# Eleven orders of the long and short products in group B of a hybrid encoder layer

## The chip, the core and the metric

The kernel runs on one core of one Trainium2 chip. The metric is the time of one execution on the device in microseconds (us); less is better. The kernel before takes 1112.13 us, the median of 3 runs (1111.66 to 1113.59).

## What is computed

One encoder layer for 256 tokens of width 2048. The input projection has nine parts of 2048 columns each; five feed group A (a gated linear recurrence), four feed group B (a short gated convolution). Cut to what matters here:

```python
hn = _rmsnorm(h, norm_w[i])                      # (256, 2048)
proj = hn @ w_in[i]                              # (2048, 9 * 2048)
q, v, f_fwd, f_bwd, z_a, b_gate, c_gate, h_b, z_b = jnp.split(proj, IN_SPLITS, axis=-1)
o_a = ...                                        # group A, from q, v, f_fwd, f_bwd, z_a
y_b = b_gate * _short_conv(c_gate * h_b, conv_w[i])
o_b = _rmsnorm(y_b, conv_norm_w[i]) * jax.nn.silu(z_b)
h = h + jnp.concatenate([o_a, o_b], axis=-1) @ w_out[i]
gate = jax.nn.sigmoid(h @ w_ple_gate[i])
h = h + (p[i] @ w_ple[i]) * gate
return _rmsnorm(h, final_norm_w)
```

## The kernel before, in words

**Products in two parts.** Every float32 matrix product is made of three products of the shorter type float32r. Both operands are split into a high part (a rounded copy) and a low part (what the rounding lost): for the weights ScalarE (ACT) makes the high part (L121) and VectorE (DVE) the low part (L122), 1024 elements of each partition at a time, into a buffer called `spl`. The activations `xs` hold high and low parts side by side, 256 columns each.

**Long and short products.** In `gemm_part` (L417 to L430) the weights are the stationary operand. For each tile of 128 inner rows (a k-tile, `kt`) and each half `m` of 256 output columns there are two matmuls. The long one (L427) has the high weights stationary and streams both parts of `xs`, 512 columns. The short one (L425) has the low weights stationary and streams the high part alone, 256 columns. Both add into the accumulator `acc[m]`, one bank of PSUM each; the short one adds to its first 256 columns. Each matmul loads its own 128x128 weights (LDWEIGHTS, on the row PEld of the profile).

**Column blocks.** `gemm_in` (L432) makes one column block: 256 columns of one part, 16 k-tiles in four groups of four (`g`, one `spl` buffer each), so 32 long and 32 short products, here called 32 pairs. Group B (L924 to L984) has 32 column blocks: for `i` from 0 to 7, one each of `B_CG`, `B_HB`, `B_BG` and `B_ZB`, named CG0, HB0, BG0, ZB0, CG1 and so on below. In all these are 1024 pairs. After each block `evac` (L482) reads the two accumulators with ACT and DVE; there are four accumulator banks, so that the next block goes on in the two others. GpSimd (POOL) and DVE do the convolution and the gates beside it.

**Order.** The order of the matmuls is that in which the program writes them. The usual order of the four products of a k-tile is PLAIN: long 0, short 0, long 1, short 1 (the number is `m`), so that long and short alternate all along. Two other orders stand at single k-tiles of some blocks, by the table TURNED: k-tile 1 by OUTER (long 0, short 0, short 1, long 1) and k-tile 3 by SHORTS (short 0, short 1, long 0, long 1). In group B TURNED stands at CG0, HB0, BG0, ZB0, CG2, CG4, CG6 and ZB6; group A has it too, and its first block has the same two orders at k-tiles 9 and 11 (LATER).

```python
PLAIN = ((0, 0), (0, 1), (1, 0), (1, 1))
OUTER = ((0, 0), (0, 1), (1, 1), (1, 0))
SHORTS = ((0, 1), (1, 1), (0, 0), (1, 0))
TURNED = {1: OUTER, 3: SHORTS}
LATER = {9: OUTER, 11: SHORTS}
```

Some small matmuls of group A's last heads stand between products of group B: those of the outputs (L797, L798) in CG0 after 24 pairs and in BG0 after 28, and the scores (L735, L779) between HB0 and BG0. Before group B stand the products of V and Z_A (`avz`, L547 to L549), which are all 512 columns long; after it those of the output projection, and last those of the gate (`pg`, L1026 to L1028), which have 512 columns, then 512 and 256 in threes, then 256 alone.

**What feeds the matmuls.** SP issues the loads of `w_in`, 1 MB each, into three buffers `raw`; ACT and DVE split them into five buffers `spl`, up to three groups ahead of the matmuls (`Stream.get`). GpSimd's queue meanwhile makes sums of parts of `w_out` in DRAM (`pump`).

Of the kernel before, what the change touches and what calls it, by code (L numbers as in the profile page):

```python
# [17 lines left out]
P = 128  # L18
D = 2048
T = 256  # L20
NKT = D // P
# [4 lines left out]
B_Q, B_V, B_FF, B_FB, B_ZA, B_BG, B_CG, B_HB, B_ZB = (8 * i for i in range(9))  # L26
# [111 lines left out]
def tile_hymba_encoder(  # L138
# [15 lines left out]
    act, dve, pool, pe = nc.scalar, nc.vector, nc.gpsimd, nc.tensor  # L154
# [16 lines left out]
    ws = Stream(tc, rawp, splp, 3)  # L171
# [5 lines left out]
    blocks = {}  # L177
# [31 lines left out]
    for u in range(2):  # L209
        for half in range(2):  # L210
            oblocks.append([])
            for q in ORDER:
                k = 16 * half + 2 * q
# [133 lines left out]
    def pump():  # L347
        if steps_up:
            n, step = steps_up.pop(0)
            add_up(prepared[n], step)  # L350
            if step == 2 and n + 4 < len(prepared):
                prepare(prepared[n + 4])

    def tick():
        now[0] += 1
        due = sorted(e for e in pend if e[0] <= now[0])
        for e in due:
            pend.remove(e)
        for e in due:
            e[2]()  # L360
# [3 lines left out]
    xs = xsp.tile([P, NKT, 2, T], F32R, name="xs")  # L364
# [42 lines left out]
    def acc_in(c, i):  # L407
        return [psg.tile([P, 2, T], F32, tag="g", name=f"a{c}_{i}_{m}") for m in range(2)]
# [5 lines that stand above are left out]
    TURNED = {1: OUTER, 3: SHORTS}  # L414
    LATER = {9: OUTER, 11: SHORTS}

    def gemm_part(acc, w, g, k0=0, k1=4, orders={}):  # L417

        for k in range(k0, k1):
            kt = 4 * g + k  # L420
            for m, short in orders.get(kt, PLAIN):
                a = acc[m].rearrange("p a b -> p (a b)")
                lhsT = w[:, k, short, m * P : (m + 1) * P]
                if short:
                    pe.matmul(a[:, :T], lhsT=lhsT, rhs=xs[:, kt, 0, :], start=False, stop=(kt == NKT - 1))  # L425
                else:
                    pe.matmul(  # L427
                        a, lhsT=lhsT, rhs=xs[:, kt, :, :].rearrange("p s n -> p (s n)"), start=(kt == 0), stop=False
                    )
            tick()  # L430

    def gemm_in(c, i, orders={}):  # L432

        acc = acc_in(c, i)
        for g in range(4):
            gemm_part(acc, ws.get(blocks[c, i][g]), g, orders=orders)
        return acc

    def gemm_two(c, i, dst):
# [42 lines left out]
    def evac(acc, dst, tmpp, offset=200):  # L482

        with tc.high_priority(offset=offset):
            for m in range(2):
                r = tmpp.tile([P, T], F32, tag="r", name="r", bufs=2)
                act.copy(out=r, in_=acc[m][:, 1, :])  # L487
                dve.tensor_tensor(out=dst(m), in0=acc[m][:, 0, :], in1=r, op=ALU.add)

    def by_norms(t, r, n):  # L490

        pool.tensor_tensor(out=t, in0=t, in1=r.unsqueeze(1).broadcast_to([P, n, T]), op=ALU.mult)  # L492


    first = (B_FF, B_FB, B_Q)
# [3 lines left out]
    with tc.manual_schedule(engines={ENG.Activation, ENG.DVE, ENG.PE}):  # L499
        for g in range(4):  # L500
            for c in range(3):
                half, v = ws.open(ids3[c][g])

                n = 2 if g or c else 1
# [24 lines left out]
    def act_sums(src, a, s, place=lambda instr: instr):  # L529


        place(dve.tensor_tensor(out=a, in0=src[:, :, 0], in1=src[:, :, 1], op=ALU.add))
        a11, a21, a12, a22 = (a[:, k, m * P : (m + 1) * P] for k in range(2) for m in range(2))
        for o, x, y in ((0, a21, a22), (1, a21, a11), (2, a11, s[:, 0]), (3, a12, s[:, 2])):
            dve.tensor_tensor(out=s[:, o], in0=x, in1=y, op=ALU.subtract)

    def act_split(dst, src, s):

        n = dst.shape[1]
        for d, r in ((dst, s[:, 0:n]), (src[:, 0:1, :, P:], s[:, n:])):  # L540
            if r.shape[1]:
                act.copy(out=d[:, :, 0], in_=r)
                dve.tensor_tensor(out=d[:, :, 1], in0=r, in1=d[:, :, 0], op=ALU.subtract)
# [374 lines left out]
    ctmp = bctx.enter_context(tc.tile_pool(name="ctmp", bufs=1, side="left", reuse_waits="tile"))  # L918
# [2 lines left out]
        pool.memset(t, 0.0)  # L921
    ysum = ctmp.tile([P, 2, T], F32, name="ysum")
    pool.memset(ysum, 0.0)
    for i in range(8):  # L924
        cg = ctmp.tile([P, 2, T], F32, tag="cg", name=f"cg{i}", bufs=2)
        evac(gemm_in(B_CG, i, TURNED if i % 2 == 0 else {}), lambda m: cg[:, m, :], ctmp)
        hb = ctmp.tile([P, 2, T], F32, tag="hb", name=f"hb{i}", bufs=2)
        evac(gemm_in(B_HB, i, {} if i else TURNED), lambda m: hb[:, m, :], ctmp)
        u = ub[i % 2]
        by_norms(cg, rbc2, 2)  # L930
        pump()
        pool.tensor_tensor(out=u[:, :, 1 : T + 1], in0=cg, in1=hb, op=ALU.mult)
        pump()
        for m in range(2):
            ct = 2 * i + m
            dve.tensor_scalar(cg[:, m, :], u[:, m, 0:T], cvw[:, 0, ct : ct + 1], None, op0=ALU.mult)
            for j in (1, 2):
                dve.scalar_tensor_tensor(
                    out=cg[:, m, :], in0=u[:, m, j : j + T], scalar=cvw[:, j, ct : ct + 1],
                    in1=cg[:, m, :], op0=ALU.mult, op1=ALU.add,  # L940
                )
        evac(gemm_in(B_BG, i, {} if i else TURNED), lambda m: hb[:, m, :], ctmp)
        pool.tensor_tensor(out=cg, in0=cg, in1=hb, op=ALU.mult)
        pump()
        y2 = ctmp.tile([P, 2, T], F32, tag="tmp", name=f"y2_{i}")
        act.activation(y2, cg, AF.Square)
        pool.tensor_tensor(out=ysum, in0=ysum, in1=y2, op=ALU.add)
        pump()
        evac(gemm_in(B_ZB, i, TURNED if i in (0, 6) else {}), lambda m: hb[:, m, :], ctmp)
        by_norms(hb, rbc, 2)  # L950
        pump()
        sz = ctmp.tile([P, 2, T], F32, tag="tmp", name=f"szb{i}")
        act.activation(sz, hb, AF.Sigmoid)
        for m in range(2):
            ct = 2 * i + m
            dve.scalar_tensor_tensor(
                out=hb[:, m, :], in0=hb[:, m, :], scalar=cnw[:, ct : ct + 1], in1=sz[:, m, :],
                op0=ALU.mult, op1=ALU.mult,
            )
        pool.tensor_tensor(out=cg, in0=cg, in1=hb, op=ALU.mult)  # L960
        pump()
        if i == 0:
            assert not pend
            actx.close()
            bp = mctx.enter_context(tc.tile_pool(name="bp", bufs=1, side="right", reuse_waits="tile"))
            mixb = bp.tile([P, NH, 2, T], F32R, name="mixb")
            og = bp.tile([P, 2, 2, 2, P], F32, name="og")
            suma = bp.tile([P, len(SUMS), 3, 2, P], F32R, name="suma")
        if i == 2:
            for e in range(2):  # L970
                act.copy(out=og[:, e], in_=kept[e])
        hi, lo = mixb[:, 2 * i : 2 * i + 2, 0, :], mixb[:, 2 * i : 2 * i + 2, 1, :]
        act.copy(out=hi, in_=cg)
        dve.tensor_tensor(out=lo, in0=cg, in1=hi, op=ALU.subtract)
        for src, z, n in ((mixa, i - 1, len(SUMS)), (mixb, i - SUMS[0], len(sumb32))):
            if 0 <= z < n:
                k = 2 * SUMS[z]
                a = ctmp.tile([P, 2, T], F32, tag="tmp", name=f"sa{i}")
                if src is mixb:
                    act_sums(mixb[:, k : k + 2], a, sumb32[z])  # L980
                else:
                    t = ctmp.tile([P, 4, P], F32, tag="hb", name=f"sb{i}", bufs=2)
                    act_sums(mixa[:, k : k + 2], a, t)
                    act_split(suma[:, z], mixa[:, k : k + 2], t)  # L984
# [22 lines left out]
    hh = hp.tile([P, 2, D], F32, name="hh")  # L1007
# [43 lines left out]
    def four(pool_, name):  # L1051
        if pool_ is psg:
            return [psg.tile([P, 512], F32, tag="g", name=f"{name}_{b}") for b in range(4)]
        return [psm.tile([P, 512], F32, tag=t, name=f"{name}_{t}") for t in FOUR]
# [8 lines left out]
    for u in range(2):  # L1063
# [9 lines left out]
        for src, sums, main, other, scale in ((mixa, suma, psg, psm, False), (mixb, sumb, psm, psg, True)):  # L1073
            name = f"p{'ab'[scale]}{u}"
            acc = four(main, name)
            parts = oblocks[2 * u + scale]
            if u == 0 and not scale:
                for z in range(len(SUMS)):
                    k = 2 * SUMS[z]
# [5 lines left out]
            for q1, q5, q6, q7 in half([acc[0:2], acc[2:4]], extra, ORDER, SUMS, parts, src, sums, False):  # L1085
                d, v, d7, v7 = tmps
# [179 lines left out]
```

## Time and profile before

| what | value |
|---|---|
| median of 3 runs | 1112.13 us (1111.66 to 1113.59) |
| the profiled execution: time, span | 1112.2 us, 1110.5 us |
| TensorE (PE) busy | 1100.5 us, 99% of the span |
| weight loads (PEld) busy | 945.7 us, 85% |
| VectorE, ScalarE, GpSimd busy | 851.4, 677.3, 269.1 us |
| mean granted clock of TensorE | 0.998 of full speed |
| chain of waits, share of PE | 98% |

The span is the time from the first to the last instruction that the profile shows; 1.7 us of the profiled execution lie around it. A matmul's row in the profile has a start and a duration; since matmuls are pipelined, durations overlap, and what a product costs in a row of them is the time from its start to the next one's start. The order of instructions is told by lists of each engine, the times by the trace.

### The profile page before, as it was taken

To read this page: it belongs to the slowest core of one execution; us is meant where nothing else is said; L and a number is where in the kernel's file an instruction comes from. 1 tells how busy PE (TensorE), PEld (TensorE's weight loads), DVE (VectorE), ACT (ScalarE), POOL (GpSimd) and SP (SyncE) were. 2 spreads that over 40 slices of the span, in tenths; PEclk is the share of its full clock that TensorE was granted. 3 is DMA by queue.
4 is the path that set the end of the run, shared out by engine and by line. 5 is a ranking of instruction groups with operands and counts; after the bars stand their busy time and mean duration, and the time that the engine had idled before them with its cause. 6 is when DMAs were issued, how large, how long until landed. Compare 5 with 4: busy or idle time off the path is not lost.

```text
span 1110.5 us, 16882 instructions
## 1 busy us (share of the span) xinstructions
PE 1100.5 (99%) x6455; PEld 945.7 (85%) x6455; DVE 851.4 (77%) x1127; ACT 677.3 (61%) x946; POOL 269.1 (24%) x215
## 2 busy tenths in 40 slices
PE   9999999999999999999999999999999999999997
PEld 8888888888888888888888888888888888888886
DVE  7799578896889778997657758856667888887673
ACT  6786577667876697575545535535546575575562
POOL 1045015203530325043334223424331000000101
PEclk9999999999999999999999999999999999999999
DMA  9755454564457744758999998999979887887542
GB/s 340 272 187 190 153 190 157 171 242 153 161 162 258 292 152 152 231 172 228 298 310 250 270 334 231 282 345 254 288 196 306 318 299 286 286 312 253 193 133 76
DMA packets 69808, 260.44 MB, mean 235 GB/s; under 512 B 7008, under 2 KB 16608, under 8 KB 52192
## 3 DMA queue, kind: packets, MB, share of 16 engines
q1 hardware_dynamic: 60480, 242.25, 62.1%
q0 software_dynamic: 8960, 16.78, 10.0%
q8 instruction: 51, 0.84, 0.3%
q10 hardware_dynamic: 288, 0.34, 0.1%
q14 instruction: 29, 0.24, 0.1%
HBM read 257.25 MB, written 35.65 MB: 264 GB/s over the span
## 4 chain that ended last, share of the span: by engine, by line
PE 98%; DMA 1%; ACT 0%; SPq 0%; DVE 0%; DVEq 0%; issue 0%; ACTq 0%
PE a L427 37%; PE a L425 19%; PE avz L547 3%; PE avz L548 3%; PE avz L549 3%; PE pg L1027 3%; PE pg L1026 3%; PE pg L1028 3%; PE pa L547 2%; PE pa L548 2%; PE pa L549 2%; PE a L446 1%; PE a L448 1%; PE a L447 1%; PE pb_sc L548 1%; PE pb_sc L549 1%
## 5 line engine op out<-in xcount | busy, mean ns | idle before, releaser
L122 DVE TENSOR_TENSOR spl<-raw,spl 128x1024 fp32r<-128x1024 f32 (+2 forms) x419 | 505.0, 1219 | 163.6 <-ACT spl L121 160.2
L427 PE MATMUL a<-xs,spl 128*128 128x512 f32 x1792 | 617.3, 395 | 0.6 <-ACT spl L121 0.6
L121 ACT CAST spl<-raw 128x1024 fp32r<-128x1024 f32 (+2 forms) x419 | 414.1, 999 | 255.0 <-PE a L425 81.9
L425 PE MATMUL a<-xs,spl 128*128 128x256 f32 x1792 | 483.8, 278 | 0.0
L427 PEld LDWEIGHTS a<-xs,spl 128*128 128x128 f32 x1792 | 332.2, 188 | 73.6 <-ACT spl L121 1.0
L425 PEld LDWEIGHTS a<-xs,spl 128*128 128x128 f32 x1792 | 334.6, 188 | 5.8 <-DVE spl L122 0.5
L1143 POOL TENSOR_TENSOR hh<-hh,fw 128x512 f32<-128x512 f32 (+1 forms) x9 | 11.0, 1227 | 250.7 <-ACT gt L1142 248.0
L487 ACT COPY r<-a 128x256 f32<-128x256 f32 x112 | 40.5, 368 | 37.3 <-PE a L425 35.8
L547 PE MATMUL avz<-spl,xs 128*128 128x512 f32 x138 | 54.0, 391 | 0.0
L549 PE MATMUL avz<-spl,xs 128*128 128x512 f32 x138 | 53.7, 389 | 0.0
L548 PE MATMUL avz<-spl,xs 128*128 128x512 f32 x138 | 53.7, 389 | 0.0
L1026 PE MATMUL pg<-spl,ht 128*128 128x512 f32 (+1 forms) x120 | 45.2, 377 | 0.0
L1027 PE MATMUL pg<-spl,ht 128*128 128x512 f32 (+1 forms) x120 | 45.1, 376 | 0.0
L1028 PE MATMUL pg<-spl,ht 128*128 128x512 f32 (+1 forms) x120 | 45.0, 375 | 0.0
L716 POOL TENSOR_TENSOR qc<-pf,ge 128x256 f32<-128x256 f32 x16 | 18.3, 1148 | 105.8 <-ACT dd L706 91.8
L492 POOL TENSOR_TENSOR xf<-xf,rbc 128x1024 f32<-128x1024 f32 x8 | 19.9, 2486 | 94.0 <-DVE rbc L403 50.2
L121 ACT CAST spl<-early 128x1024 fp32r<-128x1024 f32 (+1 forms) x29 | 28.7, 990 | 19.1 <-PE pb_y L549 7.5
L122 DVE TENSOR_TENSOR spl<-early,spl 128x1024 fp32r<-128x1024 f32 (+1 forms) x29 | 32.9, 1147 | 9.2 <-ACT spl L121 8.8
L547 PE MATMUL pa<-spl,mixa 128*128 128x512 f32 x88 | 34.5, 392 | 0.0
L549 PE MATMUL pa<-spl,mixa 128*128 128x512 f32 x88 | 34.3, 389 | 0.0
L548 PE MATMUL pa<-spl,mixa 128*128 128x512 f32 x88 | 34.2, 389 | 0.0
L716 POOL TENSOR_TENSOR kc<-dd,ge 128x256 f32<-128x256 f32 x16 | 27.7, 1728 | 19.8 <-DVE dd L707 13.6
(321 smaller groups left out, 1641.7 us busy)
## 6 DMA issues: line engine op xcount, KB each, us to landing
raw<-in_w_in_dram SPq DMA_DIRECT2D x106, 1024.0 KB, 6.9
raw<-in_w_in_dram SPq DMA_DIRECT2D x100, 256.0 KB, 3.9
raw<-in_w_out_dram SPq DMA_DIRECT2D x36, 512.0 KB, 5.2
sums<-in_w_out_dram SPq DMA_DIRECT2D x32, 512.0 KB, 10.6
raw<-in_w_in_dram SPq DMA_DIRECT2D x26, 512.0 KB, 5.2
raw<-sums SPq DMA_DIRECT2D x13, 1024.0 KB, 5.3
raw<-in_w_gate_dram SPq DMA_DIRECT2D x9, 1024.0 KB, 5.1
sums<-in_w_out_dram POOLq DMA_DIRECT2D x16, 512.0 KB, 10.1
```

The source lines that it names most:

```text
L121: self.nc.scalar.copy(out=v[:, :, 0], in_=r)
L122: self.nc.vector.tensor_tensor(out=v[:, :, 1], in0=r, in1=v[:, :, 0], op=ALU.subtract)
L425: pe.matmul(a[:, :T], lhsT=lhsT, rhs=xs[:, kt, 0, :], start=False, stop=(kt == NKT - 1))
L427: pe.matmul(a, lhsT=lhsT, rhs=xs[:, kt, :, :].rearrange("p s n -> p (s n)"), start=(kt == 0), stop=False)
L487: act.copy(out=r, in_=acc[m][:, 1, :])
L547: pe.matmul(acc, lhsT=ah, rhs=w[:, 0], start=start, stop=False)
L548: pe.matmul(acc, lhsT=ah, rhs=w[:, 1], start=False, stop=False)
L549: pe.matmul(acc, lhsT=al, rhs=w[:, 0], start=False, stop=stop)
L716: pool.tensor_tensor(out=c64(dst[:, d]), in0=c64(src[:, d, :, half * P : (half + 1) * P]), in1=g.unsqueeze(3).broadcast_to([P, 2, 2, CH]), ...
L1026: pe.matmul(acc[m], lhsT=lh, rhs=wh, start=(kt == 0), stop=False)
L1027: pe.matmul(acc[m], lhsT=lh, rhs=wl, start=False, stop=False)
L1028: pe.matmul(acc[m], lhsT=ll, rhs=wh, start=False, stop=(kt == nk - 1))
```

## The change

`gemm_part` no longer walks k-tile by k-tile with one of the three orders; it takes a list of all 16 products of a group of four k-tiles, made by `products_of` for one of eleven styles, named by letters a to k. The string STYLES gives each column block of group B its style: in turn one plain block and two blocks of one style, from CG0 (plain), HB0 and BG0 (a), ZB0 (plain), CG1 and HB1 (b), to HB7 (j), BG7 (plain) and ZB7 (k). TURNED is no longer used in group B; group A keeps it. `tick()` still comes after every four products, and the `stop` flag at the last product of each accumulator.

With L and S for long and short, the styles are: a: L0 L1 S0 S1 in each k-tile; b: L0 S1 L1 S0; c: L0 L1 S1 S0; d: in each group of four k-tiles all eight longs, then all eight shorts; e: in each group first `m` 0, then `m` 1, long and short in turn; f: in each group for each `m` four longs, then four shorts; g: by two k-tiles four longs, then four shorts; h: as d, but shorts first in the second and third groups; i: OUTER in each k-tile; j: S0 L0 S1 L1; k: SHORTS. In b, i, j and k the first and last k-tile of a block stay plain.

```diff
+    L0, S0, L1, S1 = PLAIN
+    BY_TILE = {
+        "a": (L0, L1, S0, S1), "b": (L0, S1, L1, S0), "c": (L0, L1, S1, S0),
+        "i": OUTER, "j": (S0, L0, S1, L1), "k": SHORTS,
+    }
+
+    def products_of(style, g, k0, k1, orders):
+        ks = range(k0, k1)
+        if style in ("d", "h"):
+            kinds = (1, 0) if style == "h" and 0 < g < 3 else (0, 1)
+            return [(k, m, short) for short in kinds for k in ks for m in range(2)]
+        if style == "e":
+            return [(k, m, short) for m in range(2) for k in ks for short in range(2)]
+        if style == "f":
+            return [(k, m, short) for m in range(2) for short in range(2) for k in ks]
+        if style == "g":
+            return [(k, m, short) for kk in (k0, k0 + 2) for short in range(2) for k in (kk, kk + 1) for m in range(2)]
+        plain = BY_TILE.get(style, PLAIN)
+        first = PLAIN if style in ("b", "i", "j", "k") else plain
+        return [(k, *o) for k in ks for o in orders.get(4 * g + k, plain if 0 < 4 * g + k < 15 else first)]
...
+        todo = products_of(style, g, k0, k1, orders)
...
+    STYLES = " aa bb cc dd ee ff gg hh ii jj k".ljust(32)
     for i in range(8):
         cg = ctmp.tile([P, 2, T], F32, tag="cg", name=f"cg{i}", bufs=2)
-        evac(gemm_in(B_CG, i, TURNED if i % 2 == 0 else {}), lambda m: cg[:, m, :], ctmp)
+        evac(gemm_in(B_CG, i, style=STYLES[4 * i + 0]), lambda m: cg[:, m, :], ctmp)
         hb = ctmp.tile([P, 2, T], F32, tag="hb", name=f"hb{i}", bufs=2)
-        evac(gemm_in(B_HB, i, {} if i else TURNED), lambda m: hb[:, m, :], ctmp)
+        evac(gemm_in(B_HB, i, style=STYLES[4 * i + 1]), lambda m: hb[:, m, :], ctmp)
...
-        evac(gemm_in(B_BG, i, {} if i else TURNED), lambda m: hb[:, m, :], ctmp)
+        evac(gemm_in(B_BG, i, style=STYLES[4 * i + 2]), lambda m: hb[:, m, :], ctmp)
...
-        evac(gemm_in(B_ZB, i, TURNED if i in (0, 6) else {}), lambda m: hb[:, m, :], ctmp)
+        evac(gemm_in(B_ZB, i, style=STYLES[4 * i + 3]), lambda m: hb[:, m, :], ctmp)
```

In the changed kernel the long product stands at L450 and the short one at L448. The numbers of instructions are the same on every engine; on PE the products of group B stand in another order, on DVE and ACT eight instructions have changed places with a neighbour, and on POOL and SP nothing has moved.

The first place is PE at the start of CG0, the products of its first two k-tiles; in a48_0_1, 48 is the part CG, 0 the `i`, and 1 the half `m`; 128x512 is a long and 128x256 a short product. Before:

```order
L427 MATMUL a48_0_0_4603<-xs_174,spl178_4532 128x512
L425 MATMUL a48_0_0_4603<-xs_174,spl178_4532 128x256
L427 MATMUL a48_0_1_4604<-xs_174,spl178_4532 128x512
L425 MATMUL a48_0_1_4604<-xs_174,spl178_4532 128x256
L427 MATMUL a48_0_0_4603<-xs_174,spl178_4532 128x512
L425 MATMUL a48_0_0_4603<-xs_174,spl178_4532 128x256
L425 MATMUL a48_0_1_4604<-xs_174,spl178_4532 128x256
L427 MATMUL a48_0_1_4604<-xs_174,spl178_4532 128x512
```

The second k-tile is turned (OUTER): two shorts stand in a row, then the last long, and the next product, of the third k-tile, is a long too. Now:

```order
L450 MATMUL a48_0_0_4603<-xs_174,spl178_4532 128x512
L448 MATMUL a48_0_0_4603<-xs_174,spl178_4532 128x256
L450 MATMUL a48_0_1_4604<-xs_174,spl178_4532 128x512
L448 MATMUL a48_0_1_4604<-xs_174,spl178_4532 128x256
L450 MATMUL a48_0_0_4603<-xs_174,spl178_4532 128x512
L448 MATMUL a48_0_0_4603<-xs_174,spl178_4532 128x256
L450 MATMUL a48_0_1_4604<-xs_174,spl178_4532 128x512
L448 MATMUL a48_0_1_4604<-xs_174,spl178_4532 128x256
```

CG0 now alternates from its first product to its last. The second place is PE in the first group of BG2 (part 40), one of the two blocks of style d. Now, from the fifth product on:

```order
L450 MATMUL a40_2_0_5703<-xs_174,spl218_5628 128x512
L450 MATMUL a40_2_1_5704<-xs_174,spl218_5628 128x512
L450 MATMUL a40_2_0_5703<-xs_174,spl218_5628 128x512
L450 MATMUL a40_2_1_5704<-xs_174,spl218_5628 128x512
L448 MATMUL a40_2_0_5703<-xs_174,spl218_5628 128x256
L448 MATMUL a40_2_1_5704<-xs_174,spl218_5628 128x256
L448 MATMUL a40_2_0_5703<-xs_174,spl218_5628 128x256
L448 MATMUL a40_2_1_5704<-xs_174,spl218_5628 128x256
```

Eight longs are followed by eight shorts (four of each are shown); before, this block alternated throughout. Counted over all of group B, there were 16 places where two or more shorts stand in a row, and as many with longs in a row, two of each for every TURNED; now there are 154 of each: 16 in each block of a and c, 4 in d, 8 in f and g, 3 in h, 14 in i and k, 1 in j, none in b, e and the plain ones.

## Rows read from the trace of the kernel before

**Rows 1.** The page: span, busy time of each engine, chain of waits by engine.

```profile
span 1110.5 us, 16882 instructions
...
PE 1100.5 (99%) x6455; PEld 945.7 (85%) x6455; DVE 851.4 (77%) x1127; ACT 677.3 (61%) x946; POOL 269.1 (24%) x215
...
PE 98%; DMA 1%; ACT 0%; SPq 0%; DVE 0%; DVEq 0%; issue 0%; ACTq 0%
```

**Rows 2.** Busy time by engine in group B: us, busy (count), granted clock, DMA.

```profile
474.00:836.00 362.00, 362.00 (x2180) 317.14 (x2178) 252.10 (x337) 180.84 (x260) 126.09 (x102) 1.00 0.91 265
```

**Rows 3.** Groups of instructions, 474 to 836 us: busy, mean ns, idle before, releasers.

```profile
L427 PE MATMUL a<-xs,spl 128*128 128x512 f32 x1024 | 353.6, 394 | 0.0
L425 PE MATMUL a<-xs,spl 128*128 128x256 f32 x1024 | 279.9, 277 | 0.0
...
L121 ACT CAST spl<-raw 128x1024 fp32r<-128x1024 f32 x129 | 134.4, 1050 | 103.2 <-PE a L425 65.4 <-DMA raw<-in_w_in_dram 30.4 <-PE a L427 3.7
```

**Rows 4.** Timeline of PE, plain blocks of group B: start, duration, instruction.

```profile
580.64 0.40 PE L427 MATMUL a<-xs,spl 128*128 128x512 f32 x1
...
602.83 0.40 PE L427 MATMUL a<-xs,spl 128*128 128x512 f32 x1
```

**Rows 5.** Timeline of PE, plain k-tiles of the kernel's first blocks.

```profile
14.69 0.40 PE L427 MATMUL a<-xs,spl 128*128 128x512 f32 x1
...
15.39 0.40 PE L427 MATMUL a<-xs,spl 128*128 128x512 f32 x1
15.63 0.28 PE L425 MATMUL a<-xs,spl 128*128 128x256 f32 x1
...
25.29 0.40 PE L427 MATMUL a<-xs,spl 128*128 128x512 f32 x1
```

**Rows 6.** Timeline of PE around one TURNED in group B.

```profile
657.61 0.40 PE L427 MATMUL a<-xs,spl 128*128 128x512 f32 x1
...
658.18 0.39 PE L425 MATMUL a<-xs,spl 128*128 128x256 f32 x2
...
660.40 0.40 PE L427 MATMUL a<-xs,spl 128*128 128x512 f32 x1
```

**Rows 7.** Timeline of PE, from the products of V and Z_A into CG0.

```profile
473.43 0.39 PE L549 MATMUL avz<-spl,xs 128*128 128x512 f32 x1
473.65 0.39 PE L427 MATMUL a<-xs,spl 128*128 128x512 f32 x1
...
474.35 0.40 PE L427 MATMUL a<-xs,spl 128*128 128x512 f32 x1
474.59 0.40 PE L425 MATMUL a<-xs,spl 128*128 128x256 f32 x2
```

**Rows 8.** Timeline of PE in BG0 and ZB0, after the small matmuls of the outputs.

```profile
511.95 0.40 PE L427 MATMUL a<-xs,spl 128*128 128x512 f32 x1
...
513.69 0.39 PE L427 MATMUL a<-xs,spl 128*128 128x512 f32 x1
```

**Rows 9.** Timeline of PE in the gate: products of 512 columns alone.

```profile
1061.83 0.39 PE L1026 MATMUL pg<-spl,ht 128*128 128x512 f32 x1
...
1076.11 0.39 PE L1026 MATMUL pg<-spl,ht 128*128 128x512 f32 x1
```

**Rows 10.** Timeline of PE in the gate: three of 512, three of 256, in turn.

```profile
1081.68 0.40 PE L1026 MATMUL pg<-spl,ht 128*128 128x512 f32 x1
...
1087.98 0.40 PE L1026 MATMUL pg<-held,ht 128*128 128x512 f32 x1
```

**Rows 11.** Timeline of PE in the gate: products of 256 columns alone.

```profile
1096.75 0.28 PE L1026 MATMUL pg<-spl,ht 128*128 128x256 f32 x1
...
1099.15 0.28 PE L1028 MATMUL pg<-spl,ht 128*128 128x256 f32 x1
...
1099.63 0.28 PE L1026 MATMUL pg<-held,ht 128*128 128x256 f32 x1
...
1101.75 0.28 PE L1026 MATMUL pg<-held,ht 128*128 128x256 f32 x1
```

More of the change, by code (lines that the diff above doesn't have):

```diff
@@ L415, in tile_hymba_encoder @@
     LATER = {9: OUTER, 11: SHORTS}
-    def gemm_part(acc, w, g, k0=0, k1=4, orders={}):
-        for k in range(k0, k1):
-            kt = 4 * g + k
[L421 to L430, printed above, removed]
@@ L432, in gemm_in @@
-    def gemm_in(c, i, orders={}):
+    L0, S0, L1, S1 = PLAIN
[17 more added lines that the diff above has]
+        return [(k, *o) for k in ks for o in orders.get(4 * g + k, plain if 0 < 4 * g + k < 15 else first)]
@@ new lines, in gemm_part @@
+    def gemm_part(acc, w, g, k0=0, k1=4, orders={}, style=""):
+        todo = products_of(style, g, k0, k1, orders)
+        last = {m: max(n for n, o in enumerate(todo) if o[1] == m) for m in range(2)}
+        for n, (k, m, short) in enumerate(todo):
+            kt = 4 * g + k
+            a = acc[m].rearrange("p a b -> p (a b)")
+            lhsT = w[:, k, short, m * P : (m + 1) * P]
+            stop = g == 3 and k1 == 4 and n == last[m]
+            if short:
+                pe.matmul(a[:, :T], lhsT=lhsT, rhs=xs[:, kt, 0, :], start=False, stop=stop)
+            else:
+                pe.matmul(
+                    a, lhsT=lhsT, rhs=xs[:, kt, :, :].rearrange("p s n -> p (s n)"), start=(kt == 0), stop=stop
+                )
+            if n % 4 == 3:
+                tick()
@@ L434, in gemm_in @@
+    def gemm_in(c, i, orders={}, style=""):
         acc = acc_in(c, i)
         for g in range(4):
-            gemm_part(acc, ws.get(blocks[c, i][g]), g, orders=orders)
+            gemm_part(acc, ws.get(blocks[c, i][g]), g, orders=orders, style=style)
         return acc
```

## The prediction

> **What bounds the kernel now.** I read the page first. TensorE is busy for 1100.5 of the 1110.5 us of the span, and 98% of the chain of waits is PE [rows 1]. So the time is the sum of what the products cost, one after the other, wherever PE does not wait. The busy time by stretches shows the same of group B alone: from 474 to 836 us PE is busy for all 362.00 us, at a granted clock of 1.00, with DVE at 252.10, ACT at 180.84 and POOL at 126.09 us [rows 2]. The list of instruction groups says who is ahead: ACT, which makes the high parts of the weights, idles 103.2 us in this stretch, and 65.4 us of it end when a short product frees a buffer [rows 3]. The splits wait for PE, not PE for them: neither kind of product has any idle time before it. A change in the order of products therefore acts on the time by one thing only: the time from each product's start to the next one's.
>
> The timeline of PE gives that time, and the reader should see that it is not one number. In plain blocks of group B, 64 pairs of a long and a short product take 22.19 us, 0.3467 us a pair [rows 4]. In the kernel's first blocks, with the same lines, shapes and order and 30 pairs without a wait, a pair takes 10.60/30 = 0.3533 us, and at times a short starts 0.24 us after its long (15.39 to 15.63) [rows 5]. So alternation has a **tight pace** and a **loose pace**, 6.6 ns a pair apart, and PE stays in either for as long as nothing disturbs it.
>
> **The change part by part.** It adds and removes no instruction, and leaves the queues of SP and POOL as they were, so loads and sums are issued in the same order. Eight neighbours that change places on DVE and ACT cost nothing while PE does not wait for either; if that cover went, one split of 1050 ns [rows 3] would be the size of a stall. Blocks of style h read the low halves first in two groups, and these come from DVE, after ACT's; the splits are held back by full buffers, so they lie there already. I cost this at 0. In d and h both accumulators end within the last two shorts; the next block uses the other two banks, so a later read of one delays nobody on PE. What stays are two terms.
>
> *Term 1, runs.* Places with two or more longs and shorts in a row (one run of each I call a cycle) go from 16 to 154, so 138 more. Alone, each kind is cheap: 63 long products take 14.28 us, 0.2267 each [rows 9], and shorts take 2.40/20 = 0.1200 or 2.12/18 = 0.1178 each [rows 11]. Sum of one each: 0.3445 to 0.3467, as in the tight pace or slightly less. What costs is the passage from one kind to the other. Where three of 512 and three of 256 columns take turns, 18 pairs take 6.30 us, 0.3500 a pair [rows 10]: 3.3 ns over the tight pace, 10 ns a cycle of three pairs. One TURNED holds two cycles; 8 pairs across it take 2.79 us against 8 x 0.3467 = 2.773 [rows 6], 17 ns, with the rounding of the two starts 7 to 27 ns, so 3 to 14 ns a cycle. Bounds: 0 (the price of runs alone) and 14 ns; a gain of 2.2 ns a pair is taken up as a rival. I take 10 ns, the row nearest to what is added, a steady turn of runs: 138 x 10 = **1.38 us**. The eight TURNED that go are in it, with 16 cycles.
>
> *Term 2, the pace of alternation.* Seventeen blocks still alternate throughout or nearly: the eleven plain ones and those of b, e and j, 544 pairs. Before, eight TURNED stood in their way. CG0 comes out of the products of V and Z_A, a row of longs, and its third long already takes 0.24 us (474.35 to 474.59), as in the loose pace, just ahead of the turned k-tile [rows 7]. Without it I expect CG0's first 24 pairs to stay loose, up to the small matmuls of the outputs: 24 x 6.6 ns = **0.16 us**. After such matmuls the products of BG0 and ZB0 went on at 1.74/5 = 0.348 us a pair [rows 8], near the tight pace, so the eight pairs of CG0's rest cost nothing. For the other 512 pairs the entry decides, and each comes from a new order: ZB0 to BG1 (128 pairs, out of a), HB2, CG3 to ZB3 (128, out of d), BG4, HB5, CG6, and ZB6 to BG7 (128, out of i). No row shows alternation that follows these orders. The bounds are 0 and 512 x 6.6 ns = 3.4 us. Of the two undisturbed entries that I have, one went loose [rows 7] and one near tight [rows 8], so I take half: **1.7 us**.
>
> A rule of the Trainium skill, of the page "TensorE: Matmul & The Clock Gate" (section "Back-to-back issue gap"), speaks against all of this: at full clock the gap of an isolated matmul is its columns over 2.4 GHz and 2.5 ns, whatever stands beside it. By it a pair takes an estimated 215.8 + 109.2 = 325 ns in any order, and the sum of the change is 0. The trace does not bear out the size (346.7 ns) nor that columns alone decide [rows 4, 5].
>
> The sum is 1.38 + 0.16 + 1.7 = 3.2 us. The profiled execution took 1112.2 us, 1.7 more than its span and 0.1 over the median of the runs, 1112.13. 1112.2 + 3.2 = **1115.4 us**, 0.3% slower.
>
> **The rivals.**
>
> *All entries tight.* The runs put PE in the tight pace as TURNED did. For it: a TURNED ends in a run of three longs, and the 64 pairs that I read as tight [rows 4] lie behind the one of CG2. Against it: CG0 comes out of a run of longs and is loose [rows 7], so the length or the moment of a run counts. Then only 1.38 + 0.16 us are left: 1113.7 us. It decides where fewer than about 100 of the 512 pairs are loose (below 2.2 us in all).
>
> *Order is free.* Each product costs what its columns cost in steady rows, passages come to nothing, and every entry is tight; this would be the page's rule with another constant. For it: 0.2267 + 0.1200 us of runs alone make just the 0.3467 of alternation [rows 4, 9, 11]. Against it: 0.3500 a pair where runs take turns [rows 10]. The eight TURNED give back 8 x 17 ns = 0.14 us: 1112.1 us, no slower than before. It holds if a cycle costs under 2 ns and no stretch is loose.
>
> *All entries loose, dear cycles.* 138 x 14 ns = 1.93, 0.16 and 3.4 us: 1117.7 us. For it: nothing in group B would set the pace right any more, and a loose stretch lasted for 30 pairs by itself [rows 5].
>
> *Runs are cheaper.* In long runs a pair may cost 0.3445 us [rows 9, 11], 2.2 ns less than in the tight pace. On the 256 pairs of d, f, g and h this gives 0.56 us, with the 0.14 of TURNED 0.7 us: 1111.5 us. For a gain that shows, the 480 pairs of all run styles would have to save 4.6 ns each; no row has that.
>
> That the change does not do what it says is no rival: the list of PE's instructions shows each style in its block.
>
> **How the numbers follow.** A measurement of this kernel tells about 0.2% (2.2 us) from no change, so the limit is about 1114.3 us. I give my forecast, a part of the entries loose, 0.42; all loose 0.16; both end above the limit, together 0.58 for slower. All entries tight has 0.28 and order is free 0.10, both within 0.2%; of the 0.04 of cheaper runs 0.01 stays within, so 0.39 for the same and 0.03 for faster. The predicted time is that of the forecast. The range goes from the free order, 1112.0, over the bounds of both terms to all loose, 1117.7 with 0.3 for the rounding of the rows: 1112.0 to 1118.0 us. This leaves out cheaper runs, and stalls that I cost at nothing.
>
> **What would show it.** Term 1: in blocks of a, c, f and g a pair takes near 0.350 us, and PE has no idle time before L448 and L450; at 0.3467 it was free, above 0.3515 (14 ns on a cycle of three pairs) too low. Term 2: CG0's first 24 pairs take 8.48 us instead of 8.32; plain blocks take either 11.09 or 11.31 us for 32 pairs, some of each, and a stretch keeps its pace to its end. If all take 11.09 us, the first rival holds. The prediction is wrong in kind if PE waits for a split or a load in group B, if the granted clock falls, or if the blocks of a style take a third price well outside 0.3445 to 0.3533 us a pair.

## The result and the profile after

The changed kernel takes 1115.93 us, the median of 9 runs (1115.16 to 1116.53); the kernel before, beside it, 1112.13 us (9 runs, 1111.24 to 1114.01). The ratio is 1.0031, with a 95% interval of 1.0021 to 1.0042: 3.8 us slower. The profiled execution took 1116.53 us, 4.3 more than that of the kernel before (1112.2).

The page of the changed kernel, the lines that answer to [rows 1]:

```profile
span 1114.7 us, 16881 instructions
...
PE 1104.2 (99%) x6455; PEld 947.9 (85%) x6455; DVE 854.2 (77%) x1127; ACT 676.5 (61%) x946; POOL 264.6 (24%) x215
...
PE 96%; DMA 1%; DVE 1%; ACT 1%; SPq 0%; issue 0%; POOL 0%; DVEq 0%; ACTq 0%
```

The span grew by 4.2 us and PE's busy time by 3.7, with the same 6455 matmuls. The busy time of group B, read to 840 us because it ends 3.4 us later now (columns as in [rows 2]), and then the groups of instructions of that stretch (columns as in [rows 3]):

```profile
474.00:840.00 366.00, 366.00 (x2180) 320.04 (x2179) 253.88 (x339) 180.86 (x260) 123.69 (x102) 1.00 0.90 263
```

```profile
L450 PE MATMUL a<-xs,spl 128*128 128x512 f32 x1023 | 328.5, 396 | 0.0
L448 PE MATMUL a<-xs,spl 128*128 128x256 f32 x1023 | 234.7, 280 | 0.0
...
L121 ACT CAST spl<-raw 128x1024 fp32r<-128x1024 f32 x129 | 134.3, 1051 | 108.6 <-PE a L448 53.3 <-DMA raw<-in_w_in_dram 33.1 <-PE a L450 22.0
```

The reader is to see that nothing new waits. PE is busy for all 366.00 us, the granted clock is 1.00 (the level of 2.4 GHz) as before, neither kind of product has idle time ahead of it, and ACT still idles until a product frees a buffer; in part it is now a long one (22.0 us, before 3.7), since in several styles a long ends a group. The 2048 products themselves stand further apart. From the first product of group B to its last it is 364.82 us, before 361.06: 3.76 of the 4.2 us. The rest of the program behind them takes 0.84 us more; what lies ahead, 0.36 less.

The timeline of PE of the changed kernel gives the paces: start, duration, instruction, and how often it follows itself.

```profile
512.81 0.40 PE L450 MATMUL a<-xs,spl 128*128 128x512 f32 x1
...
524.12 0.40 PE L450 MATMUL a<-xs,spl 128*128 128x512 f32 x1
...
558.04 0.62 PE L450 MATMUL a<-xs,spl 128*128 128x512 f32 x2
...
569.19 0.63 PE L450 MATMUL a<-xs,spl 128*128 128x512 f32 x2
...
580.34 0.40 PE L450 MATMUL a<-xs,spl 128*128 128x512 f32 x1
...
591.43 1.99 PE L450 MATMUL a<-xs,spl 128*128 128x512 f32 x8
593.25 1.11 PE L448 MATMUL a<-xs,spl 128*128 128x256 f32 x8
594.21 1.32 PE L450 MATMUL a<-xs,spl 128*128 128x512 f32 x5
...
602.59 0.40 PE L450 MATMUL a<-xs,spl 128*128 128x512 f32 x1
...
658.99 1.08 PE L450 MATMUL a<-xs,spl 128*128 128x512 f32 x4
659.91 0.64 PE L448 MATMUL a<-xs,spl 128*128 128x256 f32 x4
...
670.20 0.40 PE L450 MATMUL a<-xs,spl 128*128 128x512 f32 x1
```

From each block's first long to the next block's first: ZB0 (plain) 524.12 - 512.81 = 11.31 us, 0.3534 a pair, the loose pace to its last pair; HB2 (plain, the same products in the same order) 591.43 - 580.34 = 11.09 us, the tight pace of [rows 4]; ZB1 (c, runs of two) 11.15; BG2 (d, runs of eight) 11.16, and one cycle of it, 591.43 to 594.21, 2.78 us; CG4 (f, runs of four) 11.21. All 32 blocks, by the starts of their products, in ns a pair:

| blocks | ns a pair |
|---|---|
| CG0, first 24 pairs | 352.8 |
| a: HB0, BG0; c: ZB1, CG2 | 348.7, 348.4; 348.3, 348.3 |
| plain ZB0, BG1; b: CG1, HB1 | 353.5, 353.5; 353.1, 353.4 |
| plain HB2, BG4, HB5 | 346.7, 346.8, 346.8 |
| d: BG2, ZB2; h: BG5, ZB5 | 348.6, 349.2; 348.6, 348.5 |
| plain CG3, ZB3; e: HB3, BG3 | 353.5, 353.5; 353.1, 353.4 |
| f: CG4, HB4; g: ZB4, CG5 | 350.3, 350.8; 350.7, 350.8 |
| plain CG6, ZB6, BG7 | 353.5, 353.4, 353.5 |
| i: HB6, BG6; k: ZB7 | 349.0, 348.9; 348.7 |
| j: CG7, HB7 | 347.6, 353.0 |

**The sum from it.** Twelve blocks are loose: 384 pairs x 6.67 ns = 2.56 us. CG0 adds 0.15 in its first 24 pairs and 0.05 in its last eight, which are loose too (352.6 ns a pair). The blocks in runs, with CG7, stand over 32 x 346.67 ns by 1.21 us in all. The eight TURNED of the kernel before cost 0.26 us by the same count. 2.56 + 0.15 + 0.05 + 1.21 - 0.26 = 3.71 of the 3.76 us.

**Behind group B.** The waits of PE in the output projection show one stop that the kernel before does not have, a product behind a split whose load of `w_out` landed late; then the timeline of PE there:

```profile
PE pa L572 <- DVE spl L122: 0.5, 1, 0.5
```

```profile
859.99 0.39 PE L571 MATMUL pa<-spl,mixa 128*128 128x512 f32 x1
860.90 0.50 PE L572 MATMUL pa<-spl,mixa 128*128 128x512 f32 x1 [0.52 <-DVE spl L122]
861.24 0.39 PE L573 MATMUL pa<-spl,mixa 128*128 128x512 f32 x1
```

From 859.99 to 860.90 it is 0.91 us, where such a product takes 0.23: some 0.7 of the 0.84 us.

### The profile page after: what moved, and what is told of

It is laid out like the page before. It is cut to its first block, busy times and chain, and to the rows that moved or that the text cites. A ratio compares the mean times of both kernels' runs of the same rounds, so it can differ in the third digit from the quotient of the medians.

```text
span 1114.7 us, 16881 instructions
## 1 busy us (share of the span) xinstructions
PE 1104.2 (99%) x6455; PEld 947.9 (85%) x6455; DVE 854.2 (77%) x1127; ACT 676.5 (61%) x946; POOL 264.6 (24%) x215
## 4 chain that ended last, share of the span: by engine, by line
PE 96%; DMA 1%; DVE 1%; ACT 1%; SPq 0%; issue 0%; POOL 0%; DVEq 0%; ACTq 0%
PE a L450 37%; PE a L448 19%; PE avz L573 3%; PE avz L571 3%; PE avz L572 3%; PE pg L1052 3%; PE pg L1051 3%; PE pg L1053 3%; PE pa L572 1%; PE pa L573 1%; PE pa L571 1%; PE a L470 1%; PE a L471 1%; PE a L472 1%; PE pb_sc L573 1%; PE pb_sc L572 1%
## 5 line engine op out<-in xcount | busy, mean ns | idle before, releaser
L450 PE MATMUL a<-xs,spl 128*128 128x512 f32 x1792 | 592.7, 396 | 0.5 <-ACT spl L121 0.5
L448 PE MATMUL a<-xs,spl 128*128 128x256 f32 x1792 | 438.8, 279 | 0.2 <-DVE spl L122 0.2
L450 PEld LDWEIGHTS a<-xs,spl 128*128 128x128 f32 x1792 | 323.0, 188 | 62.7 <-ACT spl L121 0.8
L448 PEld LDWEIGHTS a<-xs,spl 128*128 128x128 f32 x1792 | 324.5, 188 | 18.0 <-DVE spl L122 0.5
```

The costliest lines, as they stand in the source:

```text
L450: pe.matmul(a, lhsT=lhsT, rhs=xs[:, kt, :, :].rearrange("p s n -> p (s n)"), start=(kt == 0), stop=stop)
```

## The experiments

The theory: PE alternates at one of several paces, the entry decides which, and the change pays for loose entries and, by a smaller sum, for runs. The rivals: TURNED had no part in it; the styles' runs alone cost the time; one kind of entry always gives one pace. Group B is told from its first product to its last; before takes 361.06 us there. "Pair" and "cycle" are those of the prediction.

**e1_no_turned**: the kernel before, TURNED taken out of group B, no style put in.

```diff
-        evac(gemm_in(B_CG, i, TURNED if i % 2 == 0 else {}), lambda m: cg[:, m, :], ctmp)
+        evac(gemm_in(B_CG, i), lambda m: cg[:, m, :], ctmp)
```

and the same for HB, BG and ZB.

> The kernel before with TURNED taken out of group B and nothing put in its place: all 32 blocks alternate. Theory (the pace of alternation is set by the moment at which PE enters it, and holds until the order is broken): CG0 comes out of a run of longs, so its first 24 pairs take 0.3533 us each (8.48 us, not 8.32). Small matmuls break in after these, between HB0 and BG0, and in BG0; behind the last of them 29 blocks follow without a break, from ZB0 to ZB7, and all must have one pace: either 11.09 us each, and the time is 1112.1 us, or 11.31 us each, 6.2 us more, 1118.1 us. Rival 1 (loose pairs come from what runs beside PE, the DMA traffic or the reads of the accumulators): the pace changes within these 29 blocks, and is loose at about the times at which it was in the changed kernel (512 to 558, 614 to 659, 748 to 760, 782 to 793, 804 to 827 us): 1114 to 1115 us. Rival 2 (loose pairs are the after-effect of the new orders alone): all blocks at 11.09 us, CG0 too, 1111.9 us.

Measured: 1113.6 us (10 runs), ratio 1.0007 (0.9993 to 1.0021); group B 364.16 us. CG0's first 24 pairs are loose, 352.8 ns each, so is HB0 (353.6), as TURNED's absence was to make them. But out of the small matmuls in BG0 comes a **third pace**: 230.0 ns from each long to its short and 116.7 from there to the next long, where the tight pace has 231.8 and 114.8; the sum is 346.67 in both. I call it the even pace. It holds for fourteen blocks, and then turns loose without any change of order. The timeline of this kernel at that place, all engines, and then the first longs of ZB4 and of ZB7:

```profile
674.24 1.22 DVE L122 TENSOR_TENSOR spl<-raw,spl 128x1024 fp32r<-128x1024 f32 x1
...
675.05 0.39 PE L427 MATMUL a<-xs,spl 128*128 128x512 f32 x1
675.05 0.19 PEld L425 LDWEIGHTS a<-xs,spl 128*128 128x128 f32 x1
...
675.28 0.28 PE L425 MATMUL a<-xs,spl 128*128 128x256 f32 x1
...
675.39 0.39 PE L427 MATMUL a<-xs,spl 128*128 128x512 f32 x1
...
675.51 0.19 PEld L425 LDWEIGHTS a<-xs,spl 128*128 128x128 f32 x1
675.63 0.28 PE L425 MATMUL a<-xs,spl 128*128 128x256 f32 x1
...
679.76 1.21 DVE L122 TENSOR_TENSOR spl<-raw,spl 128x1024 fp32r<-128x1024 f32 x1
...
680.95 0.39 PE L427 MATMUL a<-xs,spl 128*128 128x512 f32 x1
...
681.02 0.19 PEld L425 LDWEIGHTS a<-xs,spl 128*128 128x128 f32 x1
...
689.41 0.40 PE L427 MATMUL a<-xs,spl 128*128 128x512 f32 x1
...
825.09 0.40 PE L427 MATMUL a<-xs,spl 128*128 128x512 f32 x1
```

The weight load of a short product normally starts with the long ahead of it (675.05 and 675.05). At 675.39 the long begins a new group; the low weights of that group, from DVE, are ready at 674.24 + 1.22 = 675.46, and the load starts at 675.51, 0.12 us late. The short itself comes 232 ns after the long instead of 230: nothing that the list of waits shows. Two pairs later the pace is even again. At the next such place, a split ready at 680.97 for a long at 680.95 and a load 75 ns late, the pace becomes loose and stays so for the remaining 155 us: ZB4 to BG7, 384 pairs, take 825.09 - 689.41 = 135.68 us, 353.3 ns a pair. At the same two groups the splits lead by 1.4 us in the profiled execution of the kernel before, but by 0.95 in its second one (e7), so the lead changes from one execution to the next, and the one trace of e1 need not stand for its other nine runs. So neither value expected for the total came out, but what lies between: an entry sets the pace, it holds by itself, and at the second of two late weight loads it changed. In all twelve traces here, these are the only two late loads in alternation from ZB0 on (all others start within 6 ns of a product), and this is the only change between the tight or even and the loose pace without a change of order. That the late load is the cause is not shown: it rests on this one stretch, and the first load, later still, changed nothing that lasted. Both kernels of this comparison scattered by 6 us from run to run, so the medians say little here, and the account rests on the trace. What runs beside PE, the first rival, would have made 512 to 558 us loose as in the changed kernel; there the pace is even.

**e2_turned_back**: the changed kernel with TURNED at its eleven plain blocks.

```diff
-        evac(gemm_in(B_CG, i, style=STYLES[4 * i + 0]), lambda m: cg[:, m, :], ctmp)
+        evac(gemm_in(B_CG, i, TURNED if STYLES[4 * i + 0] == " " else {}, STYLES[4 * i + 0]), lambda m: cg[:, m, :], ctmp)
```

> The changed kernel with TURNED at k-tiles 1 and 3 of each of the eleven plain blocks, the 21 blocks of styles a to k as they are. Theory: TURNED brings each stretch to 0.3467 us a pair from its second k-tile on, also the blocks of b, e and j that follow one. Twelve blocks and 24 pairs of CG0 were loose: 2.56 + 0.16 us go, eleven TURNED cost 11 x 0.026 = 0.29 us: 2.4 us less than the changed kernel, 1113.5 us. Rival 1 (what runs beside PE): plain blocks stay at 11.31 us where they were, and the time is 1116.2 us. Rival 2 (the runs themselves are the cost): the run blocks keep their 348 to 351 ns a pair in both theories, but then the plain blocks would not matter: less than 0.5 us of change.

Measured: 1113.73 us (10 runs), ratio 1.0005 (0.9994 to 1.0017); group B 362.41 us. Plain blocks take 347.4 to 348.4 ns a pair with their TURNED in it, b and e 346.7, HB7 346.8 (loose in the changed kernel: 353.0); the blocks in runs stay at 348.0 to 350.8. The timeline of PE of this kernel, the first longs of CG1 and of BG1:

```profile
522.95 0.39 PE L450 MATMUL a<-xs,spl 128*128 128x512 f32 x1
...
545.14 0.39 PE L450 MATMUL a<-xs,spl 128*128 128x512 f32 x1
```

The two blocks of style b take 22.19 us, where the changed kernel takes 22.61 for the same products in the same order. 2.41 of the 3.76 us are gone, with every style still in place. So the larger part of the loss was the pace between the runs. What is left, 1.35 us, is the price of the runs and that of TURNED itself, at eleven blocks instead of eight.

**e3_a_c_swapped**: the changed kernel, styles a and c exchanged.

```diff
-    STYLES = " aa bb cc dd ee ff gg hh ii jj k".ljust(32)
+    STYLES = " cc bb aa dd ee ff gg hh ii jj k".ljust(32)
```

> The changed kernel with styles a and c in each other's blocks: c in HB0 and BG0, a in ZB1 and CG2. They differ in which of the two shorts comes first (S0 S1 or S1 S0), so in which accumulator follows which, and in nothing of the sizes. Theory (sizes and moments alone): everything as before the swap: ZB0 to BG1 loose (11.31 us), HB2 tight (11.09), run blocks at 348.3 to 348.7 ns a pair, the same time within 0.2 us plus noise. Rival (the style or the accumulator decides what follows): ZB0 to BG1 tight and HB2 loose, 3 x 0.21 = 0.64 us less in group B.

Measured once: 1115.94 us; group B 364.82 us, to the hundredth that of the change. ZB0 to BG1 are loose out of c as they were out of a, and HB2 is tight behind a as behind c. Which accumulator the last short goes to does not matter here. What differs between the two places is the stream ahead of the runs; the next experiment tells how that enters.

**e4_single_tiles**: the kernel before with one turned k-tile in each of 28 blocks, of four kinds (TURNED only in the first four blocks).

```diff
+    TILES = {"o": OUTER, "s": SHORTS, "a": (L0, L1, S0, S1), "j": (S0, L0, S1, L1)}
+    SINGLE = "---- o5s5a5j5 o6s6a6j6 o7s7a7j7 o8s8a8j8 o5o6o5o6 s5s6s5s6 a5a6a5a6".split()
...
-        evac(gemm_in(B_CG, i, TURNED if i % 2 == 0 else {}), lambda m: cg[:, m, :], ctmp)
+        evac(gemm_in(B_CG, i, one_tile(0, i)), lambda m: cg[:, m, :], ctmp)
```

> The kernel before, but in each of the 28 blocks from CG1 to ZB7 exactly one k-tile (number 5, 6, 7 or 8) has another order: OUTER, SHORTS, L0 L1 S0 S1 or S0 L0 S1 L1; CG0 to ZB0 keep TURNED. So 28 single breaks with at least seven k-tiles of alternation on each side. Theory: the pace changes at the breaks only; between two breaks it is one of 0.3467 and 0.3533 us (or near 0.3468 as after f and g), and what comes out depends on the kind of break and on the moment (phase) at which it falls, so that the same kind at an odd and an even k-tile, or out of a tight and a loose stretch, can end differently. Time: 1112 us and up to 28 x 0.21 = 6 us. Rival 1: changes of pace between the breaks. Rival 2: one kind of break always brings the tight pace and another always the loose one.

Measured once: 1115.23 us; group B 363.91 us. The pace changed at those k-tiles and nowhere else. The pace behind each, by the pace ahead of it (number of places):

| k-tile | out of tight | out of even | out of loose |
|---|---|---|---|
| OUTER | even 1 | loose 5 | loose 1, even 1 |
| SHORTS | loose 1 | tight 2 | loose 3, even 1, tight 1 |
| a | loose 3 | | tight 4, loose 1 |
| j | even 3 | | even 1 |

Out of the tight or the even pace one kind of k-tile always led to the same one (OUTER and SHORTS out of the tight pace stand there only once each); out of the loose pace it did not. So the rival that one kind of k-tile leads to one pace falls.

The trace shows more. The loose pace is a pattern of three pairs, from long to short and on to the next long 233 + 117, 241 + 120 and 236 + 113 ns, and what comes out of it goes with the pair of the pattern that stands just ahead of the k-tile:

| k-tile out of the loose pace | behind 233 + 117 | behind 241 + 120 | behind 236 + 113 |
|---|---|---|---|
| OUTER | loose 1 | | even 1 |
| SHORTS | tight 1 | loose 3 | even 1 |
| a | tight 4 | loose 1 | |
| j | | | even 1 |

The timeline of PE around the k-tile of style a in HB7, then a long behind it and the one three pairs later, and the same in BG7:

```profile
807.12 0.40 PE L427 MATMUL a<-xs,spl 128*128 128x512 f32 x1
...
807.48 0.63 PE L427 MATMUL a<-xs,spl 128*128 128x512 f32 x2
...
808.53 0.40 PE L427 MATMUL a<-xs,spl 128*128 128x512 f32 x1
...
809.59 0.40 PE L427 MATMUL a<-xs,spl 128*128 128x512 f32 x1
```

```profile
817.72 0.40 PE L427 MATMUL a<-xs,spl 128*128 128x512 f32 x1
...
818.07 0.64 PE L427 MATMUL a<-xs,spl 128*128 128x512 f32 x2
...
819.13 0.39 PE L427 MATMUL a<-xs,spl 128*128 128x512 f32 x1
...
820.17 0.40 PE L427 MATMUL a<-xs,spl 128*128 128x512 f32 x1
```

In HB7 the pair ahead takes 0.36 us, and three pairs behind the k-tile take 1.06 us: loose. In BG7 the pair ahead takes 0.35 us, and three pairs behind take 1.04 us: tight. Two cells of the table hold more than one place, seven in all, without an exception; the others stand once each, so the rule fits every place but is little tested. The expectation had named the moment of the break as what might decide. TURNED, an OUTER and then a SHORTS, is by this table tight to even and back to tight, which fits the one pace of [rows 4] in all later blocks of the kernel before.

**e6_all_c**: the changed kernel, all 32 blocks of style c.

```diff
-    STYLES = " aa bb cc dd ee ff gg hh ii jj k".ljust(32)
+    STYLES = "c" * 32
```

> The changed kernel with style c (L0 L1 S1 S0) in all 32 blocks of group B. The four blocks of a and c took 348.3 ns a pair in the changed kernel, whatever pace they came out of. Theory: runs of two have one pace of their own, so all 32 blocks take 11.15 us (348.3 ns a pair), CG0 too; group B is 1024 x 1.67 ns = 1.7 us over undisturbed tight alternation and 1.5 us over the kernel before with its TURNED: 1113.6 us (against 1112.1 of before). Rival (runs too have several paces, set by the entry): some blocks at another price, 350 ns or more a pair, and up to 3.5 us over before.

Measured: 1113.63 us (10 runs), ratio 1.001 (1.0001 to 1.0019); group B 362.49 us. The timeline of PE of this kernel, the first longs of CG1 and of ZB7, 27 blocks apart:

```profile
523.48 0.63 PE L450 MATMUL a<-xs,spl 128*128 128x512 f32 x2
...
824.44 0.63 PE L450 MATMUL a<-xs,spl 128*128 128x512 f32 x2
```

300.96 us for 27 x 32 pairs, 348.3 ns each: one price, no loose stretch. A cycle of runs of two costs 2 x 1.67 = 3.3 ns.

**e9_one_shorts** and **e10_one_outer**: e1 with one turned k-tile more in the whole of group B, the sixth of CG1; the kernels differ in that k-tile's order alone.

```diff
-        evac(gemm_in(B_CG, i, TURNED if i % 2 == 0 else {}), lambda m: cg[:, m, :], ctmp)
+        evac(gemm_in(B_CG, i, {5: SHORTS} if i == 1 else {}), lambda m: cg[:, m, :], ctmp)
```

with OUTER for SHORTS in the second.

> The kernel before without TURNED in group B (as e1_no_turned), and one single k-tile in the whole group in another order: number 5 of CG1 by SHORTS. In e1_no_turned the pace from ZB0 on had longs of 230.0 and shorts of 116.7 ns (346.7 ns a pair) until a split came late at 676 to 681 us. In e4_single_tiles SHORTS turned this pace into that of 231.8 and 114.8 ns (also 346.7) both times. Theory: the same here: 27 blocks at 11.09 us with 231.8 and 114.8 ns; if that pace stands a late split, to the end of the group: 1112.1 us, no slower than before. Rival (one k-tile changes nothing, a late split loosens the pace as in e1_no_turned): 353 ns a pair from about 680 us on, 1114 us.

> As e9_one_shorts, but the single k-tile (number 5 of CG1) by OUTER. In e4_single_tiles OUTER turned the pace of 230.0 and 116.7 ns into the loose one all five times. Theory: from there on 27 blocks and 20 pairs at 353.3 ns a pair, 884 x 6.67 ns = 5.9 us more than with the tight pace: 1118 us, 0.5% slower than before, by the order of four products out of 2048. Rival (the pace comes from elsewhere): the same as e9_one_shorts.

The timeline of PE with SHORTS, the first longs of HB1 and of ZB7:

```profile
534.13 0.39 PE L427 MATMUL a<-xs,spl 128*128 128x512 f32 x1
...
822.56 0.39 PE L427 MATMUL a<-xs,spl 128*128 128x512 f32 x1
```

and with OUTER:

```profile
533.93 0.40 PE L427 MATMUL a<-xs,spl 128*128 128x512 f32 x1
...
827.91 0.40 PE L427 MATMUL a<-xs,spl 128*128 128x512 f32 x1
```

26 blocks are 832 pairs: 288.43 us, 346.7 ns a pair, against 293.98 us, 353.3 ns. With SHORTS the kernel takes 1112.4 us (10 runs), ratio 1.0002 (0.999 to 1.0013), with OUTER 1117.77 us (5 runs), ratio 1.0045 (1.0031 to 1.0059); group B takes 361.24 and 367.11 us. One k-tile's order is worth 5.9 us of group B, since the pace it sets is kept to the end; the table of e4 forecast both outcomes. The even pace of e1 is gone too: with SHORTS PE stays at 231.8 and 114.8, or 231.5 and 115.2, through the place where e1 turned loose, and the splits lead there: the one of the group that begins at 675.57 is ready at 674.07, so this run does not try the late load. The time with SHORTS holds a stop of the kind told above, in the output projection.

**e7_before_again** is the kernel before, unchanged.

> The kernel before once more, as a second trace of it. The changed kernel and the four others profiled so far had a stop of 0.4 to 0.9 us in the output projection, some 20 us behind group B, where PE waits for a split whose load landed late; the one trace of before had none, but the split ended there in the same moment in which PE wanted it. If this stop is chance in the landing of a load, it stands in this trace too, and the rest behind group B takes 276.2 to 276.6 us instead of 275.7; if it comes with the new orders, it is missing again. Group B itself: 361.1 us from its first to its last product, as in the first trace.

Measured once: 1111.09 us, group B 361.06 us again, without a stop behind it.

**e8_late_split**: the kernel before, with four idle multiplications on DVE in CG4, to make splits late in the tight pace.

```diff
+        if i == 4:
+            for _ in range(4):
+                dve.tensor_scalar(cg, cg, 1.0, None, op0=ALU.mult)
```

> The kernel before with four more instructions on DVE in CG4: cg multiplied by 1.0 four times (about 0.5 to 0.9 us each), which puts off the splits of the next groups. In the kernel before these were ready 1.4 us or more ahead of PE at their latest (HB4 and BG4). Theory: PE waits for one or two low halves in HB4 or BG4, up to 2 us in all; and if a late split can also break the pace of 231.8 and 114.8 ns, the blocks behind it are loose until CG6's TURNED (5 to 6 blocks, 1.1 to 1.3 us more); if that pace stands it, they stay at 11.09 us. Both are open; in e1_no_turned the pace of 230.0 and 116.7 ns did not stand it.

Measured once: 1111.54 us, group B 361.06 us. A miss: the four instructions took 0.42 us each, between 677.48 and 680.44 us, and the splits still led by 1.53 us or more, so nothing was late. Whether the tight pace would stand a late weight load stays open.

**e5_four_turned**: the kernel before, TURNED only in the first four blocks.

```diff
-        evac(gemm_in(B_CG, i, TURNED if i % 2 == 0 else {}), lambda m: cg[:, m, :], ctmp)
+        evac(gemm_in(B_CG, i, {} if i else TURNED), lambda m: cg[:, m, :], ctmp)
```

> The kernel before without the four later TURNED (CG2, CG4, CG6, ZB6); those of CG0, HB0, BG0 and ZB0 stay. Theory: ZB0's TURNED leaves the pace of 231.8 and 114.8 ns, and nothing disturbs it, so 28 blocks stay at 11.09 us and the four places give back 4 x 26 ns = 0.1 us: 1112.0 us, the same as before. Rival (the later ones are needed): a stretch loosens on its own somewhere between CG2 and ZB7, 0.2 us a block, up to 5 us.

Measured: 1111.82 us (10 runs), ratio 1.0004 (0.9994 to 1.0013); group B 360.96 us. From CG1 on all blocks take 11.09 us, the later four TURNED gave nothing, and to leave them out saves 0.10 us, less than a measurement can tell.

## Why the prediction came out as it did

**What bounds the kernel**: right. In group B PE waits for nothing that the lists of waits show, in the changed kernel as before, and the time moved with the distance of the products alone. The exchange of neighbours on DVE and ACT and the reading of low halves first in h were costed at nothing, and cost nothing in group B.

**Term 1, runs**: the mechanism was right, the size was not. The prediction took 10 ns a cycle for all, from the runs of three of [rows 10], 1.38 us with TURNED subtracted. The runs came to 1.21 - 0.26 = 0.95 us. A cycle of runs of two (a, c) cost 3.3 ns where c stood alone, one of i or k 4.6 to 5.3; a cycle of four and four (f, g) 15 to 17, of eight and eight (d) or eight and sixteen (h) 16 to 20. The row of three and three lies between these; most of the added cycles are of two. The expected 0.350 us a pair was seen in f and g, while a and c took 0.348. TURNED, read as 17 ns each, cost about twice that, 0.26/8 = 33 ns, of which the four later ones took 27 to 30 each.

**Term 2, the pace**: right that entries would split and that CG0 would be loose (8.47 us for its 24 pairs, 8.48 forecast, 0.15 us). CG0's last eight pairs, costed at nothing from [rows 8], were loose too, 0.05 us. Too low was the share: "so I take half", 1.7 us; it was 384 of 512 pairs, three quarters, 2.56 us. Two earlier entries are too few to give a share. That "a stretch keeps its pace to its end" held for ZB0 to BG1 and CG3 to ZB3, but not for ZB6 to BG7: CG7 is tight between loose neighbours. Style j alternates inside, but has two shorts in a row at its second k-tile and two longs in a row at its last; in CG7 the pace turned at the first of these places and turned back at the other. Out of a, d, h and i the plain blocks were loose, out of c tight, out of f and g even; why, no run here takes apart, and e3 shows only that a and c may change places.

The errors went opposite ways, 0.4 us too much and 0.9 too little, so the sum of 3.2 us was near the 3.71 counted. The forecast of 1115.4 us stands beside a median of 1115.93, and its range holds it. The mechanism was right; that the sum came this near is in part luck, since the half rested on one entry of either kind and the two errors happened to cancel.

**What was left out**: the stop in the output projection, "stalls that I cost at nothing", some 0.7 us in the profiled execution. The load in question lands, by the end of ACT's wait for it, 19.2 to 19.6 us after the start of group B's last product in the four traces without a stop (before, e5, e7, e8) and 20.0 to 21.0 in the eight with one (the change and the other experiments); the stops cost 0.4 to 1.4 us. e9, with group B as fast as before, has one too, so the time of group B does not explain it. What makes that load late stays open.

**The rivals.** All entries tight, 1113.7 us: close to what e2 gives by restoring TURNED, 1113.73, and not what the change does. Order is free and runs are cheaper: out, by e6 (348.3 ns a pair in runs of two with nothing else in the way) and by every run style over 346.67. All entries loose: e10 is nearly that case for one alternation throughout, 1117.77 us, and the change has four of its sixteen blocks tight or even.

The Trainium skill's rule that was weighed there, in "TensorE: Matmul & The Clock Gate" (section "Back-to-back issue gap"), gives the gap of an isolated matmul by its columns; of a stream of weight loads and matmuls the same section of the Trainium skill says that both set the spacing, so the prediction carried the rule further than it goes. e9 and e10 speak against it as a rule for this stream: the same products, with the same columns, in the same order but for one k-tile, took 346.7 and 353.3 ns a pair at the same granted clock, 1.00.

## What to carry to other kernels

Where PE never waits, read the distance of the products block by block, not the busy share: a steady stream of two sizes can run at several paces, 2% apart here, and the order of four products can choose one for hundreds of microseconds (e9, e10). A turned k-tile that looks useless (TURNED) may be what sets the pace; if it is taken out or moved, look at the pace behind it before the price of the thing itself. Such a pace may be fragile: in e1 it was lost where a weight load came 75 ns late, though no list of waits showed it. That keeping the splits well ahead of the products protects it is a guess that no run here tried.

## What the runs showed of the hardware that was not expected

The paces repeat from run to run. By the starts of products, from long to short and from short to long: tight, a pattern of two pairs, on average 231.8 and 114.8 ns (in some blocks 231.5 and 115.2); even, the same in each pair, 230.0 and 116.7; loose, a pattern of three pairs, 233, 241 and 236 ns from long to short and 117, 120 and 113 from short to long, on average 353.3 a pair. In all three each weight load starts 1 to 6 ns after the start of a product. The same alternating products can thus settle into periods of one, two or three pairs, and the third costs 6.7 ns a pair. The pace behind a single turned k-tile followed in e4, in all 28 places, from the kind of k-tile, the pace ahead and, out of the loose pace, the pair of the pattern just ahead. What in TensorE makes these patterns no run here shows. That runs of four cost about 4 ns a pair and runs of two or eight only about 2 was not expected either, and its cause was not tried.
